# GpSimd multiplies x by 1/rms and ScalarE makes h twice in the first stage; six more filling products at the beginning

## The chip, the cores and the metric

The kernel runs on one core of a Trainium2 chip. The metric is the device time of one execution in microseconds. Before the change three runs gave a median of 972.54 us (971.67 to 973.52). One further execution was profiled; its instructions can be read one by one.

The engines of a core work side by side, each through its own list of instructions in order: TensorE (PE, matrix products; PEld is its weight load), VectorE (DVE), ScalarE (ACT), GpSimd (POOL), and SyncE (SP), which here only issues DMAs. An instruction waits until the semaphores that it names are reached, and everything behind it on its engine waits with it.

## The reference, cut to what matters

A decoder trunk of two layers. Each layer has a feed-forward network (FFN), a token mixer (attention) and a second FFN. Before each of them x is normalised and modulated with a scale and a shift that come from the vector c:

```
def rms_norm(x, g):
    xf = x.astype(jnp.float32)
    y = xf * lax.rsqrt(jnp.mean(xf * xf, axis=-1, keepdims=True) + EPS)
    return (y * g.astype(jnp.float32)).astype(x.dtype)

def modulate(h, shift, scale):
    return h * (1 + scale[:, None, :]) + shift[:, None, :]

def swiglu(h, w_in, w_out):
    g, u = jnp.split(h @ w_in, 2, axis=-1)
    return (jax.nn.silu(g) * u) @ w_out

        mod = c_act @ ada_w[layer] + ada_b[layer]
        sh1, sc1, g1, sh2, sc2, g2, sh3, sc3, g3 = jnp.split(mod, N_MOD, axis=-1)
        h = modulate(rms_norm(x, norm_g[layer, 0]), sh1, sc1)
        x = x + 0.5 * g1[:, None, :] * swiglu(h, ffn_w_in[layer, 0], ffn_w_out[layer, 0])
```

x has 256 positions and 1024 features, the hidden width of the FFN is 2816, and everything is float32. The change concerns the first of these stages alone: h of layer 0's first FFN, with A = g x (1 + scale) and the shift sh, h = x x (1/rms) x A + sh.

## The kernel before

x lies in SBUF with features on the 128 partitions: eight blocks k = 0 to 7 of 128 features by 256 positions. A float32 product is made of three products of reduced precision: each operand is split into a high half and the rest. Of h these are the tiles `HH` and `HL`, of the weights `wh` and `wl`, and `mm3` (line 410) issues wh·HH, wl·HH and wh·HL, in this order, so the third product of each group needs `HL`.

Weights come from HBM through SP's queue in pieces of 128 by 1024 into `raw` (six buffers). ScalarE casts a piece to its high half `wh` (`cp_part`, line 298, six buffers), and VectorE subtracts to get `wl` (`sub_part`, line 310, five buffers); the subtraction frees the `raw` buffer, and SP issues the next load. The modulation is computed on VectorE: `ada_block` (line 196) multiplies a loaded tile `ada` of 128 by 1024 with `cact` and sums over the free axis into one column of `modall`. The block of a scale is followed by a tiny operation that makes the column of A; the block of a shift gives its column directly.

The beginning (lines 900 to 926) loads x, squares it on ScalarE, sums over the features with products against a tile of ones (`psn`), and `rstd_of` (line 452) makes r = 1/rms of it with one ScalarE operation and three on VectorE. `warm(n)` (line 893) issues n products of the ones with themselves; their results are used by nobody. Then the first stage of the FFN begins (line 573). For every block k of x it does, in the order of the code:

- for k > 0: `ada_block` (scale column k), `cp_part`, `ada_block` (shift column k);
- `make_h` (line 467): VectorE makes `ht` = x·A·r in one operation, ScalarE makes `HH` = ht + sh in its high half;
- `sub_part` and `cp_part`: `wl` of the step's first weight piece, `wh` of its second;
- the function that `make_h` returned: VectorE makes `HL` = ht + sh - HH;
- `sub_part`: `wl` of the second piece;
- 16 blocks of weight columns through `mm3`: 48 products of 128x256 into the eight PSUM banks `pf0` to `pf7`.

One such pass is called a step here; the eight steps make the stage. The order on each engine is the order of this code; TensorE goes from step to step as the tiles become ready. Behind the stage the banks are emptied (`evac`: ScalarE's `sg`, VectorE's `hf` and `hidl`, ScalarE's `hidh`), and the next groups of hidden columns go to the banks `pg` and `pu`. For the rest of the kernel a small planner (class `InOrder`, line 54, and `bg`, `fill_act`, `fill_dve`) decides, from estimated costs, between which products a cast, a subtraction or an `ada_block` is placed.

Of the kernel before, what the change touches and what calls it, by code (L numbers as in the profile page):

```python
# [10 lines left out]
F32 = mybir.dt.float32  # L11
F32R = mybir.dt.float32r
BF16 = mybir.dt.bfloat16
AF = mybir.ActivationFunctionType
ALU = mybir.AluOpType
PSUM = bass.MemoryType.PSUM

P = 128
D = 1024
S = 256  # L20
NC = D // P
# [82 lines left out]
def trunk(ctx, tc, a, out):  # L104
    nc = tc.nc
    InOrder.ready = {}
    pe = InOrder(tc, nc.tensor, 0.0, 1 / 2350)
    act = InOrder(tc, nc.scalar, 0.13, 1 / 1200)
    dve = InOrder(tc, nc.vector, 0.08, 1 / 960)
    sp = InOrder(tc, nc.sync, 0.0, 1 / 704)  # L110
    cp_ = ctx.enter_context(tc.tile_pool(name="cp", bufs=1))
# [3 lines left out]
    kp = ctx.enter_context(tc.tile_pool(name="kp", bufs=2))  # L115
    pp = ctx.enter_context(tc.tile_pool(name="pp", bufs=1, space=PSUM))

    def mmbank(name):
        return pp.tile([P, 512], F32, tag="mm", name=name, bufs=4)

    def sbank(name):
        return pp.tile([P, 512], F32, tag="s", name=name, bufs=2)

    def abank(name):
        return pp.tile([P, 512], F32, tag="ta", name=name)

    def bbank(name):
        return pp.tile([P, 512], F32, tag="tb", name=name)
# [17 lines left out]
    x = [xx[:, k] for k in range(NC)]  # L146
# [17 lines left out]
    def table(func):  # L164
        act.preload_act_table(func)


    mods = {}
# [27 lines left out]
    def ada_block():  # L196

        u, i = divmod(ada_done[0], 2)
        if u >= len(ada_list):
            return  # L200
        ada_done[0] += 1
        t = ada_tiles[u]
        m, j = ada_list[u][i]
        if m not in mods:
            mods[m] = [mod_col(), None]
        mt = mods[m][0]
        col = V_ADAB + 2 * u + i
        dve.tensor_tensor_reduce(
            t[:, i], t[:, i], cact, 1.0, vecs[:, col:col + 1], ALU.mult, ALU.add,
            accum_out=mt[:, j:j + 1])  # L210
        kind = m[1] % 3 if m[0] != "kv" else m[1]
        if kind != 0 and m[1] != 5:
            if mods[m][1] is None:
                mods[m][1] = mod_col()
            mx = mods[m][1]
            js = (j, j + 1) if m == (0, 1) else ((j - 3, j + 1) if j % 4 == 3 else None)
            if js is not None:
                js = slice(*js)
                if kind == 1:
                    gc = V_KVN if m[0] == "kv" else V_NORM + (m[0] * 3 + m[1] // 3) * NC  # L220
                    dve.scalar_tensor_tensor(
                        mx[:, js], mt[:, js], 1.0, vecs[:, gc + js.start:gc + js.stop],
                        op0=ALU.add, op1=ALU.mult)
                else:
                    dve.tensor_scalar_mul(mx[:, js], mt[:, js], 0.5)
        if i == 1:
            ada_dma()
# [70 lines left out]
    def cp_part():  # L298

        u = len(his)  # L300
        n = pieces[u][2]
        act.t = max(act.t, used[u - NHI] if u >= NHI else 0.0)
        raw = raws[u]
        if u >= len(pieces) - 6:
            gated[0](raw[:, :n])
        wh = wp.tile([P, WB], F32R, tag="wh", name="wh")[:, shift.get(u, 0):]
        act.plainly(lambda: act.copy(wh[:, :n], raw[:, :n]))
        his.append(wh)

    def sub_part():  # L310

        u = len(los)
        if u == len(his):
            return
        n = pieces[u][2]
        dve.t = max(dve.t, used[u - NLO] if u >= NLO else 0.0)
        wl = wp.tile([P, WB], F32R, tag="wl", name="wl", bufs=NLO)[:, shift.get(u, 0):]
        dve.plainly(lambda: dve.tensor_tensor(wl[:, :n], raws[u][:, :n], his[u][:, :n].bitcast(F32),
                                              op=ALU.subtract))
        los.append(wl)  # L320
        w_dma()
# [80 lines left out]
    def later(n, f):  # L402
        laters.append([n, f])
# [6 lines left out]
    def mm3(ps, w, xx, first, last):  # L410
        (wh, wl), (xh, xl) = w, xx
        mm(ps, wh, xh, start=first, stop=False, skip_group_check=True)
        mm(ps, wl, xh, start=False, stop=False, skip_group_check=True)
        mm(ps, wh, xl, start=False, stop=last, skip_group_check=True)
        work(P)
# [5 lines left out]
    hn = [(HH[:, k, :S], HL[:, k, :S]) for k in range(NC)]  # L421
# [45 lines left out]
    def make_h(k, r, m):  # L467

        A, sh = mods[m[0]][1], mods[m[1]][0]
        t = kp.tile([P, S], F32, tag="ht", name=f"ht{k}")  # L470
        dve.scalar_tensor_tensor(t, x[k], A[:, k:k + 1], r, op0=ALU.mult, op1=ALU.mult)
        hh, hl = hn[k]
        act.activation(hh, t, AF.Identity, bias=sh[:, k:k + 1])
        return lambda: dve.scalar_tensor_tensor(hl, t, sh[:, k:k + 1], hh.bitcast(F32),
                                                op0=ALU.add, op1=ALU.subtract)

    class MakeH:


# [68 lines left out]
    def ffn(l, i, kind, m, nxt, at=2):  # L548
# [24 lines left out]
        if (l, i) == (0, 0):  # L573
            banks = ([mmbank(f"pf{b}") for b in range(4)] + [sbank(f"pf{b}") for b in range(4, 6)]
                     + [abank("pf6"), bbank("pf7")])
            for k in range(NC):
                if k:
                    ada_block()
                    cp_part()
                    ada_block()  # L580
                f = make_h(k, kind, m)
                sub_part()
                cp_part()
                f()
                sub_part()
                blk = take("win0")
                for b in range(4 * K0):
                    mm3(banks[b // 2][:, (b % 2) * 256:(b % 2) * 256 + 256], blk(b * P), hn[k],
                        k == 0 and b % 2 == 0, k == NC - 1)
            table(AF.Silu)  # L590
            cp_part()
            sub_part()
            cp_part()
            sub_part()
            mode[0] = "run"
            for j in range(K0):
                if j < 2:
                    evac(banks[2 * j], banks[2 * j + 1])
                    if j == 0:
                        flush()  # L600
                        flush()
                else:
                    later(2 * j - 2, lambda j=j: evac(banks[2 * j], banks[2 * j + 1]))
            j0 = K0
        elif kind == "late":
            banks = [mmbank("lg0"), mmbank("lg1"), sbank("lu0"), sbank("lu1")]
            r = None
            for kh in range(2):
                blk = take("win")
                for kk in range(4):  # L610
                    k = kh * 4 + kk
                    for b in range(4):
                        mm3(banks[b][:, :SX], blk(kk * 512 + b * P), hx[k], k == 0, k == NC - 1)
                    if k == 2:
                        r = rstd_of(AF.Silu)
                        mh = MakeH(r, m)
                    elif 2 < k < 7:
                        mh.go(2 if k < 6 else 1)
            mh.go(2)
            mode[0] = "run"  # L620
            sg = kp.tile([P, 512], F32, tag="w512a", name="sg")
            hf = kp.tile([P, 512], F32, tag="w512b", name="hf")
            cols = []

            def late_block(b):
                if b == 0:
                    cols.append(late_cols(banks))
                c = cols[0]
                t = kp.tile([P, S], F32, tag="sq", name=f"lt{b}")
                dve.tensor_tensor(t, banks[b][:, :S], r, op=ALU.mult)  # L630
                cs = slice((b % 2) * S, (b % 2) * S + S)
                if b < 2:
                    act.activation(sg[:, cs], t, AF.Silu, bias=c[:, b:b + 1])
                else:
                    dve.scalar_tensor_tensor(hf[:, cs], t, c[:, b:b + 1], sg[:, cs],
                                             op0=ALU.add, op1=ALU.mult)
                if b == 3:
                    hid_out(hf)
            for b in range(4):
                later(2 + b, lambda b=b: late_block(b))  # L640
            j0 = 1
        for j in range(j0, NG):
            pg, pu = mmbank(f"pg{j}"), mmbank(f"pu{j}")
            for kh in range(2):
                blk = take("win")
                for kk in range(4):
                    k = kh * 4 + kk
# [14 lines left out]
        for n in range(NC):  # L662
# [3 lines left out]
            for hf in range(2):  # L666
                blk = take("wout")
                for kk in range(11):
                    k = hf * 11 + kk
# [3 lines left out]
                    hh, hl = hid[k // 2]  # L673
# [219 lines left out]
    def warm(n):  # L893

        pw = bbank("warm")
        for _ in range(n):
            mm(pw[:, :P], ones, ones, start=True, stop=True)
# [24 lines left out]
    ada_block()  # L922
    ada_block()
    rstd = rstd_of(None, [sq4[i][:, h * S:(h + 1) * S] for i in (0, 2) for h in range(2)])
    warm(6)
    cp_part()


# [226 lines left out]
    op, rest = attention_a()  # L1155
# [212 lines left out]
    op, rest = attention_b()  # L1368
# [132 lines left out]
```

## Time and profile before

| | |
|---|---|
| median of three runs | 972.54 us |
| lowest and highest | 971.67 and 973.52 us |
| the profiled execution | 974.37 us, of which 972.5 us are its span (first to last instruction) |
| mean granted clock of TensorE in it | 0.996 |
| PE busy over the span | 960.3 us, 99% |
| DVE busy | 821.7 us, 84% |
| ACT busy | 552.1 us, 57% |
| POOL busy | 68.7 us, 7% |

A row of a timeline gives the start and the duration in microseconds, the engine, the line (99 for all instructions that go through the recording class `InOrder`), the operation, what it writes and reads, how many instructions are merged in it, and in brackets the idle time before it with what ended it. Matmuls are pipelined: their starts are the measure of their pace, and their recorded durations overlap. The rows of busy time by stretch give, after the stretch, the busy time of PE, PEld, DVE, ACT and POOL with the number of instructions, the granted TensorE clock, the busy share of the DMA engines and GB/s. `CUSTOM_DVE_ANT_0` is VectorE's product with a sum behind it, and `DVE_READ_ACCUMULATOR2_ANT` writes that sum out.

### The profile page before, as it was taken

The page shows a single profiled execution, that of the slowest core. Times are in us where ns is not written, and L with a number is a line of the kernel's source. Part 1 is how long each engine was busy: PE and PEld are TensorE (multiplying, and loading weights), DVE is VectorE, ACT ScalarE, POOL GpSimd, SP SyncE. Part 2 cuts the span into 40 slices and gives each one's busy share as a digit, 9 for nine tenths or more (in the row PEclk, how much of TensorE's full clock was granted, in tenths as well). Part 3 has the DMA queues.
Part 4 walks back from the last instruction along what each step waited for, and adds up shares of the span by engine and source line. Part 5 has one row for each costly group of instructions (what it writes and reads, how often), then busy time and mean ns, then how long its engine had stood idle before and what let it go on. Part 6 is the DMA issues. An engine that isn't in the chain of part 4 may idle for free.

```text
span 972.5 us, 20416 instructions
## 1 busy us (share of the span) xinstructions
PE 960.3 (99%) x8076; PEld 933.7 (96%) x8076; DVE 821.7 (84%) x1372; ACT 552.1 (57%) x894; POOL 68.7 (7%) x110
## 2 busy tenths in 40 slices
PE   8999999999999999999999999999999999999997
PEld 6999999998999999999998999999998899999997
DVE  6988979889999999888889988988988799555575
ACT  5366645566787654545577555445567676455432
POOL 0000200000112000000000000000044014300000
PEclk9999999999999999999999999999999999999999
DMA  9997899968856699878959799988895337978651
GB/s 357 415 356 248 333 371 350 332 234 257 333 182 258 190 374 382 334 253 315 326 190 380 280 348 329 371 290 318 321 313 171 109 110 223 273 151 275 186 152 44
DMA packets 69473, 268.22 MB, mean 276 GB/s; under 512 B 9417, under 2 KB 10225, under 8 KB 59266
## 3 DMA queue, kind: packets, MB, share of 16 engines
q1 hardware_dynamic: 66016, 259.69, 75.9%
q0 software_dynamic: 3072, 6.92, 2.4%
q8 instruction: 63, 1.03, 0.4%
q10 hardware_dynamic: 290, 0.32, 0.1%
q14 instruction: 32, 0.26, 0.1%
HBM read 264.75 MB, written 2.66 MB: 275 GB/s over the span
## 4 chain that ended last, share of the span: by engine, by line
PE 96%; DVE 2%; DMA 1%; ACT 0%; issue 0%; SPq 0%; ACTq 0%
PE po L99 25%; PE pg L99 21%; PE pu L99 21%; PE pf L99 5%; PE pv L99 5%; PE pw L99 4%; PE lp L99 4%; PE pqk L99 3%; PE lg L99 1%; PE lq L99 1%; PE lu L99 1%; PE pk L99 1%; PE wb L99 1%; DVE ada L99 1%; DMA x<-in_x 1%; PE sb L99 1%
## 5 line engine op out<-in xcount | busy, mean ns | idle before, releaser
L99 ACT CAST wh<-raw 128x1024 fp32r<-128x1024 f32 (+1 forms) x360 | 347.1, 975 | 211.1 <-PE pu L99 76.8
L99 DVE TENSOR_TENSOR wl<-raw,wh 128x1024 fp32r<-128x1024 f32 (+1 forms) x360 | 399.6, 1128 | 68.9 <-ACT sg L99 19.0
L99 DVE CUSTOM_DVE_ANT_0 ada<-ada,cact,vecs 128x1024 f32<-128x1024 f32 x160 | 203.3, 1277 | 0.0
L99 PE MATMUL pg<-HH,wl 128*128 128x256 f32 x608 | 168.1, 277 | 0.4 <-DVE wl L99 0.4
L99 PE MATMUL pg<-HH,wh 128*128 128x256 f32 x608 | 168.0, 276 | 0.0
L99 PE MATMUL pg<-HL,wh 128*128 128x256 f32 x608 | 167.9, 276 | 0.0
L99 PE MATMUL pu<-HH,wh 128*128 128x256 f32 x608 | 167.9, 276 | 0.0
L99 PE MATMUL pu<-HL,wh 128*128 128x256 f32 x608 | 167.9, 276 | 0.0
L99 PE MATMUL pu<-HH,wl 128*128 128x256 f32 x608 | 167.9, 276 | 0.0
L99 PE MATMUL po<-hidh,wh 128*128 128x256 f32 x528 | 145.7, 276 | 0.0
L99 PE MATMUL po<-hidh,wl 128*128 128x256 f32 x528 | 145.7, 276 | 0.0
L99 PE MATMUL po<-hidl,wh 128*128 128x256 f32 x528 | 145.7, 276 | 0.0
L99 PEld LDWEIGHTS pg<-HH,wl 128*128 128x128 f32 x608 | 114.1, 188 | 0.9 <-DVE wl L99 0.8
L99 PEld LDWEIGHTS pg<-HH,wh 128*128 128x128 f32 x608 | 114.1, 188 | 0.7 <-issue 0.6
L99 PEld LDWEIGHTS pu<-HH,wl 128*128 128x128 f32 x608 | 114.1, 188 | 0.0
L99 PEld LDWEIGHTS pg<-HL,wh 128*128 128x128 f32 x608 | 114.1, 188 | 0.0
L99 PEld LDWEIGHTS pu<-HH,wh 128*128 128x128 f32 x608 | 114.1, 188 | 0.0
L99 PEld LDWEIGHTS pu<-HL,wh 128*128 128x128 f32 x608 | 114.1, 188 | 0.0
L99 PEld LDWEIGHTS po<-hidl,wh 128*128 128x128 f32 x528 | 99.1, 188 | 0.0
L99 PEld LDWEIGHTS po<-hidh,wh 128*128 128x128 f32 x528 | 99.1, 188 | 0.0
L99 PEld LDWEIGHTS po<-hidh,wl 128*128 128x128 f32 x528 | 99.1, 188 | 0.0
L99 ACT CAST hidh<-hf 128x512 fp32r<-128x512 f32 x44 | 27.3, 621 | 41.7 <-DVE hf L99 41.7
(224 smaller groups left out, 1855.0 us busy)
## 6 DMA issues: line engine op xcount, KB each, us to landing
raw<-in_win SPq DMA_DIRECT2D x176, 512.0 KB, 6.8
ada<-in_ada SPq DMA_DIRECT2D x79, 1024.0 KB, 7.2
raw<-in_wout SPq DMA_DIRECT2D x48, 384.0 KB, 5.5
raw<-in_wout SPq DMA_DIRECT2D x48, 320.0 KB, 5.3
raw<-in_wqk SPq DMA_DIRECT2D x16, 512.0 KB, 5.6
raw<-in_wo SPq DMA_DIRECT2D x16, 512.0 KB, 5.2
raw<-in_wlast SPq DMA_DIRECT2D x16, 512.0 KB, 4.2
raw<-in_wv SPq DMA_DIRECT2D x8, 512.0 KB, 6.2
```

Of the source, the lines that this page charges most:

```text
L99: return self.tc.keep_in_program_order(f(*args, **kw))
```

## The change

In the first stage, for the blocks k = 1 to 7, the product x·r is taken from VectorE and made by GpSimd, all seven right behind one another as soon as r exists, into seven tiles `xr` that borrow the memory of the later `hidh1` to `hidh7`. ScalarE then computes A·xr + sh twice: once into `HH` (high half), once into `ht` in float32. VectorE's operation for `HL` becomes a plain subtraction, ht - HH. Block 0 is made as before. The filling products before the stage become twelve instead of six.

```
+    def spread_r(k, r):
+
+        xr = cp_.tile([P, 512], F32, tag=f"hidh{k}", name=f"xr{k}")[:, :S]
+        nc.gpsimd.tensor_tensor(xr, x[k], r, op=ALU.mult)
+        return xr
+
+    def make_h_from(k, xr, m):
+
+        A, sh = mods[m[0]][1], mods[m[1]][0]
+        hh, hl = hn[k]
+        act.activation(hh, xr, AF.Identity, bias=sh[:, k:k + 1], scale=A[:, k:k + 1])
+        t = kp.tile([P, S], F32, tag="ht", name=f"ht{k}")
+        act.activation(t, xr, AF.Identity, bias=sh[:, k:k + 1], scale=A[:, k:k + 1])
+        return lambda: dve.tensor_tensor(hl, t, hh.bitcast(F32), op=ALU.subtract)
+
...
-                f = make_h(k, kind, m)
+                if k == 0:
+                    f = make_h(k, kind, m)
+                    xrs = [None] + [spread_r(j, kind) for j in range(1, NC)]
+                else:
+                    f = make_h_from(k, xrs[k], m)
                 sub_part()
                 cp_part()
                 f()
...
-    warm(6)
+    warm(12)
```

The first place is VectorE's list from `ht` of step 0 to the end of step 1, before the change (`ISA ada` is the product with a sum of an `ada_block`, `ISA modall` the row that writes the sum out):

```order
L99 SCALAR_TENSOR_TENSOR ht_171<-x,modall,r_148 128x256
L99 TENSOR_TENSOR wl<-raw,wh 128x1024
L99 SCALAR_TENSOR_TENSOR HL<-ht_171,modall,HH 128x256
L99 TENSOR_TENSOR wl<-raw,wh 128x1024
L99 ISA ada,modall<-ada,cact,vecs 128x1024
L99 ISA modall 128x1
L99 SCALAR_TENSOR_TENSOR modall<-modall,vecs 128x1
L99 ISA ada,modall<-ada,cact,vecs 128x1024
L99 ISA modall 128x1
L99 SCALAR_TENSOR_TENSOR ht_240<-x,modall,r_148 128x256
L99 TENSOR_TENSOR wl<-raw,wh 128x1024
L99 SCALAR_TENSOR_TENSOR HL<-ht_240,modall,HH 128x256
```

and the same stretch after it, from the first `ada` sum of step 1 on:

```order
L99 ISA ada,modall<-ada,cact,vecs 128x1024
L99 ISA modall 128x1
L99 SCALAR_TENSOR_TENSOR modall<-modall,vecs 128x1
L99 ISA ada,modall<-ada,cact,vecs 128x1024
L99 ISA modall 128x1
L99 TENSOR_TENSOR wl<-raw,wh 128x1024
L99 TENSOR_TENSOR HL<-ht_261,HH 128x256
L99 TENSOR_TENSOR wl<-raw,wh 128x1024
```

`ht` of step 1 has left VectorE's list, and `HL` reads two tiles and no column; so in each of the steps 1 to 7, and nothing else has moved on this engine.

The second place is ScalarE's list from `HH` of step 0 to that of step 2, before the change (a row with x2 is the second piece of one step and the first of the next):

```order
L99 ACTIVATE HH<-ht_171,modall 128x256
L99 CAST wh<-raw 128x1024 x2
L99 ACTIVATE HH<-ht_240,modall 128x256
L99 CAST wh<-raw 128x1024 x2
L99 ACTIVATE HH<-ht_309,modall 128x256
```

and after it (the numbered `xr` are GpSimd's products):

```order
L99 ACTIVATE HH<-ht_177,modall 128x256
L99 CAST wh<-raw 128x1024 x2
L99 ACTIVATE HH<-xr_180,modall 128x256
L99 ACTIVATE ht_261<-xr_180,modall 128x256
L99 CAST wh<-raw 128x1024 x2
L99 ACTIVATE HH<-xr_182,modall 128x256
L99 ACTIVATE ht_330<-xr_182,modall 128x256
```

`ht` now stands between `HH` and the cast of the step's second weight piece.

The third place is GpSimd's list behind the program's start, where there was nothing ahead of `udram` before; after the change:

```order
L480 ISA
L480 TENSOR_TENSOR xr_180<-x,r_148 128x256
L480 TENSOR_TENSOR xr_182<-x,r_148 128x256
L480 TENSOR_TENSOR xr_184<-x,r_148 128x256
L480 TENSOR_TENSOR xr_186<-x,r_148 128x256
L480 TENSOR_TENSOR xr_188<-x,r_148 128x256
L480 TENSOR_TENSOR xr_190<-x,r_148 128x256
L480 TENSOR_TENSOR xr_192<-x,r_148 128x256
L970 DMA udram<-ut 8x383
```

The seven products stand one behind the other. On TensorE only the number of filling products differs, and SP's list is the same as before.

## The prediction

> **What bounds the kernel now.** I read the page's chain of work first, then the PE's own timeline at the beginning, then the stages' busy time with the granted clock, and last VectorE's and ScalarE's timelines in the first stage.
>
> ```profile
> PE 96%; DVE 2%; DMA 1%; ACT 0%; issue 0%; SPq 0%; ACTq 0%
> ```
>
> The time is TensorE's time: 96% of the chain that ended last. An edit in the first stage counts only by what it does to the moment at which TensorE leaves that stage. So the PE timeline there, from the filling products to the first product of the next stage:
>
> ```profile
> 11.18 1.50 PE L99 MATMUL warm<-ones 128*128 128x128 f32 x12
> 15.19 0.38 PE L99 MATMUL pf<-HH,wh 128*128 128x256 f32 x1 [2.51 <-ACT HH L99]
> 15.79 0.38 PE L99 MATMUL pf<-HH,wl 128*128 128x256 f32 x1 [0.21 <-DVE wl L99]
> 16.18 0.55 PE L99 MATMUL pf<-HL,wh 128*128 128x256 f32 x1
> ...
> 62.70 0.28 PE L99 MATMUL pf<-HL,wh 128*128 128x256 f32 x1
> 62.82 0.27 PE L99 MATMUL pg<-HH,wh 128*128 128x256 f32 x1
> ```
>
> TensorE stands still for 2.5 us, starts at 15.19, is held once for the first `wl` and once for the first `HL`, and runs without a break from 16.18 to 62.82. Its pace in that run, by busy time in stretches (the second of these rows counts the products of the stage alone; the column behind the counts is the granted clock):
>
> ```profile
> 16.25:19.66 3.41, 3.41 (x16) 3.41 (x17) 3.38 (x5) 1.04 (x1) 0.00 (x0) 0.50 1.00 414
> 25.00:60.00 35.00, 35.00 (x300) 1.00 1.02 413
> ```
>
> In the second row 300 products touch 35.0 us, the two at the edges only in part: one per 0.1175 us, so a step of 48 takes 5.64 us. In the first row the clock is half: 3.41 us give the work of 1.7 us. The half clock follows the pause at 12.7 to 16.2, and it costs 1.7 us. Check: 16.18 + 46 x 0.1175 + 1.7 + 7 x 5.64 = 62.8, as seen.
>
> VectorE runs beside it. One step, then the last `HL` of the stage:
>
> ```profile
> 13.65 0.42 DVE L99 SCALAR_TENSOR_TENSOR r<-ra,r 128x256 f32<-128x256 f32 x1
> 14.11 0.48 DVE L99 SCALAR_TENSOR_TENSOR ht<-x,modall,r 128x256 f32<-128x256 f32 x1
> 14.51 1.22 DVE L99 TENSOR_TENSOR wl<-raw,wh 128x1024 fp32r<-128x1024 f32 x1
> 15.65 0.48 DVE L99 SCALAR_TENSOR_TENSOR HL<-ht,modall,HH 128x256 fp32r<-128x256 f32 x1
> 16.11 1.23 DVE L99 TENSOR_TENSOR wl<-raw,wh 128x1024 fp32r<-128x1024 f32 x1
> 17.25 1.28 DVE L99 CUSTOM_DVE_ANT_0 ada<-ada,cact,vecs 128x1024 f32<-128x1024 f32 x1
> ...
> 19.86 0.08 DVE L99 DVE_READ_ACCUMULATOR2_ANT modall<- 128x1 f32 x1
> 19.86 0.48 DVE L99 SCALAR_TENSOR_TENSOR ht<-x,modall,r 128x256 f32<-128x256 f32 x1
> 20.25 1.22 DVE L99 TENSOR_TENSOR wl<-raw,wh 128x1024 fp32r<-128x1024 f32 x1
> 21.39 0.48 DVE L99 SCALAR_TENSOR_TENSOR HL<-ht,modall,HH 128x256 fp32r<-128x256 f32 x1
> 21.85 1.23 DVE L99 TENSOR_TENSOR wl<-raw,wh 128x1024 fp32r<-128x1024 f32 x1
> ...
> 55.83 0.48 DVE L99 SCALAR_TENSOR_TENSOR HL<-ht,modall,HH 128x256 fp32r<-128x256 f32 x1
> ```
>
> VectorE has no idle time here, and its step is (55.83 - 21.39) / 6 = 5.74 us, longer than TensorE's 5.64. It does not hold TensorE, because TensorE lost 1.7 us to the clock: the last step starts at 62.82 - 5.64 = 57.18, wants `HL` with its third product at 57.4, and `HL` is there at 56.31. The margin is 1.1 us, less than the 1.7 us of the clock. So neither edit alone could bring all of it.
>
> **The change part by part.**
>
> *The six fillers.* Twelve records took 1.50 us, so twelve more run from 12.68 to about 14.1, before `HH` lets the first product go at 15.19. They delay nothing. If they keep the clock, step 0 ends at 16.18 + 46 x 0.1175 = 21.6 instead of 23.3. No row shows how much work keeps it, so the value lies between 0 and -1.7 us.
>
> *VectorE's part.* Seven `ht` go, 0.40 us each by the starts 19.86 and 20.25. Seven `HL` become plain subtractions, for which the nearest row is this one:
>
> ```profile
> 967.16 0.41 DVE L99 TENSOR_TENSOR x<-x,rows 128x256 f32<-128x256 f32 x1
> ```
>
> That is 0.07 us less than 0.48. Counted from the end of the second `ada` sum, `HL` comes 0.47 us earlier, and VectorE's own work per step falls to some 5.2 us. That gain meets a new wait.
>
> *ScalarE's part.* The same `ht` now stands on ScalarE, between `HH` and the cast of the step's second weight piece:
>
> ```profile
> 20.37 0.51 ACT L99 ACTIVATE HH<-ht,modall 128x256 fp32r<-128x256 f32 x1 [1.86 <-DVE ht L99]
> 20.79 1.03 ACT L99 CAST wh<-raw 128x1024 fp32r<-128x1024 f32 x1
> ```
>
> `HH` needs the shift column, so it can start when the accumulator is read, 19.94 + 0.04. Then `HH` 0.42 (start to start), `ht` the same, the cast 1.03 and 0.04 for the signal: the second `wl` can start at 21.89. Before it starts at 21.85. VectorE's step therefore stays at 5.78 us: it now ends with a wait on ScalarE's cast, and queued behind that waiting `wl` are both `ada` sums on which the next `HH` depends. It is a ring through both engines; the removed 0.5 us turn into idle time. What is left of the gain is `HL` 0.47 us earlier within the step.
>
> *GpSimd's part.* Seven multiplies are queued without a wait between them, and they ask from about 14.15, when r is there (13.65 + 0.42). No row shows them in this stage. Elsewhere GpSimd multiplies or adds tiles of the same size, beside VectorE:
>
> ```profile
> 58.66 2.36 DVE L99 TENSOR_TENSOR wl<-raw,wh 128x1024 fp32r<-128x1024 f32 x2 [1.14 <-ACT wh L99]
> 723.34 2.89 DVE L99 TENSOR_TENSOR wl<-raw,wh 128x1024 fp32r<-128x1024 f32 x2
> 724.28 0.87 POOL L1253 TENSOR_TENSOR d<-d,tri 128x256 f32<-128x256 f32 x1 [1.65 <-DMA d<-fdram]
> 779.95 0.73 POOL L448 TENSOR_TENSOR acc<-sq,sq 128x256 f32<-128x256 f32 x1 [24.45 <-ACT sq L99]
> 780.00 0.97 DVE L99 SCALAR_TENSOR_TENSOR HL<-x,modall,HH 128x256 fp32r<-128x256 f32 x1
> 741.29 1.42 POOL L1253 TENSOR_TENSOR d<-d,tri 128x256 f32<-128x256 f32 x2 [2.79 <-DMA d<-fdram]
> 741.30 0.42 DVE L99 CUSTOM_DVE_ANT_0 d<-sb,d 128x256 f32<-128x256 f32 x1
> ```
>
> Two `wl` with a GpSimd operation between them take 2.89 us instead of 2.36, and that operation 0.87 instead of 0.73: it waited for the first `wl` to finish, then the second `wl`, already queued, waited for it. An `HL` begun 0.05 us behind a GpSimd operation takes 0.97 instead of 0.48. So the two take turns, and one GpSimd operation costs a busy VectorE about 0.53 us. In the last two rows nothing is lost: that VectorE operation reads `sb` from PSUM, and `d` alone from SBUF. In the first stage VectorE's operations read two tiles from SBUF and stand back to back, so a GpSimd operation slips in at nearly each change. For the `ada` sum (`ada` and `cact`, both in SBUF) no row has it beside such a multiply: between 0, as for `d<-sb,d`, and 0.53, as for `wl`, I take 0.53, since its operands lie as those of `wl`.
>
> The Trainium skill, "SBUF — State Buffer", section "Who interferes with whom", says that a VectorE instruction with two SBUF inputs contends with a GpSimd instruction that reads SBUF, and that the lock holds for the whole instruction. The rows above agree (0.53 and 0.49 us); by that rule the `ada` sum is held too, and the sum stays as it follows here.
>
> Up to `HL` of step 1 there are the changes ht/wl, wl/HL, HL/wl, wl/ada, ada/modall, modall/ada and wl/HL: seven for seven multiplies. The tiny `modall` operation and the sum behind it lie closer together than GpSimd's cadence of about 0.7 us, so one may be saved; I take six and a half, 3.45 us, between 0 (all hidden) and 3.7.
>
> *The sum at TensorE.* The first `HL` comes two holds later, so the unbroken run starts at 16.18 + 1.06 = 17.24, and step 0 ends at 22.65 with the full clock, at 24.35 with the half. `HL` of step 1 is ready at 21.87 - 0.47 + 3.45 = 24.85; a step's first two products (0.235 us) do not need it, so step 1 starts at 24.85 + 0.05 - 0.235 = 24.67 either way. That is the point: TensorE waits there for VectorE, and what the fillers save is waited away. In step 1 the holds hide the cast, so `HL` of step 2 follows after 5.26, then five times 5.78: 59.0 for the last one. Step 7 starts at 58.8 (TensorE alone would be at 24.67 + 6 x 5.64 = 58.5) and ends at 64.45, against 62.82: **+1.6 us**.
>
> Behind the stage the shift has to pass one narrow place:
>
> ```profile
> 57.58 2.00 ACT L99 CAST wh<-raw 128x1024 fp32r<-128x1024 f32 x2
> 60.94 0.68 DVE L99 TENSOR_TENSOR hf<-sg,pf 128x512 f32<-128x512 f32 x1
> ```
>
> `hf` empties the second bank at 61.6, and TensorE wants it six products after 62.82, at 63.5. That margin of 1.9 us shrinks to a few tenths, since ScalarE's line there moves by some 3.2 us and TensorE's by 1.6; I cost it at nothing, and up to 0.5 if it is gone. After that TensorE is the chain again and carries 1.6 us to the end. The profiled execution took 974.37 us (span 972.5 and 1.9 around it) and would become 976.0. It lies 1.8 us above the median of the runs, 972.54, a difference that I carry over: 972.54 + 1.6 = **974.2 us**.
>
> **The rivals.**
>
> *A: as summed.* 974.2 us, with six or seven holds and the narrow place 973.8 to 975.0. For it: the turns at 723 and 780.
>
> *B: the `ada` sum is not held.* Only three holds lie on the path, 1.6 us: `HL` of step 1 at 23.0, the last at 57.7. TensorE ends at 63.1 with the full clock, or at 24.35 + 7 x 5.64 = 63.8 with the half: +0.3 to +1.0, some 973.2. For it: the 0.42 us at 741.30; against it: that one reads PSUM.
>
> *C, the slower side: the clock falls once more.* If the fillers keep the clock at first, TensorE stands from 22.65 to 24.67. The clock fell after a pause of 2.5 us with two short ones behind it; a pause of 2.0 us may do it too. Then another 1.7 us go, with no margin to absorb them: 975.9. It decides if a pause of 2.0 us is enough. The Trainium skill, "TensorE: Matmul & The Clock Gate", section "Why this matters for your kernels", warns of pauses over about 3 us; by that rule C does not occur, but the trace disagrees, with half clock after 2.5 us.
>
> *D: GpSimd costs nothing.* The last `HL` comes at 21.40 + 6 x 5.78 = 56.1, TensorE ends at 61.55 with the full clock: -1.3, 971.3. Against it: the pairs of rows above.
>
> *E: the change does what it says.* No holds and no ring: VectorE's step falls to 5.2, TensorE alone decides, 21.6 + 7 x 5.64 = 61.1: -1.7, 970.8. Against it: the holds and the cast behind `ht`. That VectorE is relieved in fact is the claim that I doubt.
>
> **How the numbers follow.** A 0.48, B 0.13, C 0.17, D 0.12, E 0.10. About 0.2%, 1.95 us, is what a measurement of this kernel tells from no change. Slower by more: C, and about four tenths of A, whose upper part lies over 974.5 and more so where the runs before had kept their clock: 0.36. Faster by more: only E with a lucky start, 0.06. Within: 0.58. The range goes from D, 971.3, to C, 975.9; E's end and the worst of C are left out.
>
> **What would show it.** GpSimd's multiplies from 14.15 to about 24, several of them well over 0.73 us; the first `wl` at about 1.75 us; TensorE's run from 17.2; a wait of TensorE on `HL` before 24.9; VectorE idle for ScalarE's cast in each later step, with 5.78 us from `HL` to `HL`; the first product of `pg` at 64.4. It is wrong if the `ada` sums keep 1.28 us beside GpSimd (B), if a second stretch of half clock shows after 23 (C), or if `pg` starts before 62.8 (D, E).

## The result and the profile after

| | before | after |
|---|---|---|
| median of six runs | 972.24 us | 976.80 us |
| lowest and highest | 971.67 and 973.52 us | 976.53 and 980.92 us |
| the profiled execution | 974.37 us, span 972.5 | 980.92 us, span 979.1 |

The kernel became slower: the ratio of after to before is 1.0052, with a 95% interval from 1.0035 to 1.0069, that is by 3.4 to 6.7 us. The forecast was 974.2 us, at most 975.9. Ratios here and below are estimated from all the runs and differ a little from the quotient of the medians. One run of the kernel before, among the 35 beside e1 to e4, took 1775.31 us at a granted clock of 0.80; it counts neither in the ratios nor in the spread given below.

The page's chain of the changed kernel, by engine:

```profile
PE 88%; DVE 7%; ACT 2%; DMA 2%; issue 1%; SPq 0%; ACTq 0%; DVEq 0%
```

TensorE had 96% of the chain and VectorE 2%; now VectorE has 7%. The chain goes through VectorE in the first stage, with ScalarE's cast once in each later step, to 59.6 us, and through TensorE from there on. The PE timeline of the changed kernel (start, duration, what; in brackets the idle time before and what ended it) begins and leaves the stage like this:

```profile
14.35 0.39 PE L99 MATMUL pf<-HH,wh 128*128 128x256 f32 x1 [1.39 <-ACT HH L99]
15.47 0.38 PE L99 MATMUL pf<-HH,wl 128*128 128x256 f32 x1 [0.74 <-DVE wl L99]
16.34 0.58 PE L99 MATMUL pf<-HL,wh 128*128 128x256 f32 x1 [0.49 <-DVE HL L99]
...
65.17 0.27 PE L99 MATMUL pg<-HH,wh 128*128 128x256 f32 x1
```

Starts of two executions can't be compared as they stand, since r is ready at another moment in each (loads at the beginning): 14.07 us in the profile of before, 12.25 + 0.42 = 12.67 here. So the measure used from here on is the **stretch**, from the end of r to the first product of `pg`: 62.82 - 14.07 = 48.75 us before, 65.17 - 12.67 = 52.50 us after. VectorE's timeline of the changed kernel shows where it went:

```profile
12.25 0.42 DVE L99 SCALAR_TENSOR_TENSOR r<-ra,r 128x256 f32<-128x256 f32 x1
12.71 1.05 DVE L99 SCALAR_TENSOR_TENSOR ht<-x,modall,r 128x256 f32<-128x256 f32 x1
13.68 1.74 DVE L99 TENSOR_TENSOR wl<-raw,wh 128x1024 fp32r<-128x1024 f32 x1
15.34 0.94 DVE L99 SCALAR_TENSOR_TENSOR HL<-ht,modall,HH 128x256 fp32r<-128x256 f32 x1
16.21 1.75 DVE L99 TENSOR_TENSOR wl<-raw,wh 128x1024 fp32r<-128x1024 f32 x1
17.88 1.75 DVE L99 CUSTOM_DVE_ANT_0 ada<-ada,cact,vecs 128x1024 f32<-128x1024 f32 x1
19.56 0.07 DVE L99 DVE_READ_ACCUMULATOR2_ANT modall<- 128x1 f32 x1
19.67 0.57 DVE L99 SCALAR_TENSOR_TENSOR modall<-modall,vecs 128x1 f32<-128x1 f32 x1
20.17 1.84 DVE L99 CUSTOM_DVE_ANT_0 ada<-ada,cact,vecs 128x1024 f32<-128x1024 f32 x1
21.94 0.08 DVE L99 DVE_READ_ACCUMULATOR2_ANT modall<- 128x1 f32 x1
21.94 1.22 DVE L99 TENSOR_TENSOR wl<-raw,wh 128x1024 fp32r<-128x1024 f32 x1
23.24 0.42 DVE L99 TENSOR_TENSOR HL<-ht,HH 128x256 fp32r<-128x256 f32 x1
24.17 1.23 DVE L99 TENSOR_TENSOR wl<-raw,wh 128x1024 fp32r<-128x1024 f32 x1 [0.51 <-ACT wh L99]
25.32 1.28 DVE L99 CUSTOM_DVE_ANT_0 ada<-ada,cact,vecs 128x1024 f32<-128x1024 f32 x1
...
29.23 0.43 DVE L99 TENSOR_TENSOR HL<-ht,HH 128x256 fp32r<-128x256 f32 x1
...
59.15 0.42 DVE L99 TENSOR_TENSOR HL<-ht,HH 128x256 fp32r<-128x256 f32 x1
```

Two things are to be seen. From 12.71 to 22 seven operations of VectorE each take some half a microsecond more than their like at other times, `ada` too (1.75 and 1.84, against 1.28 at 25.32): the holds. Only the reading of the accumulator is not longer (0.07). From `HL` of step 2 at 29.23 to that of step 7 at 59.15 there are five steps of 5.98 us; before, a step took 5.74. GpSimd's timeline and the waits of VectorE between 20 and 62 us (total, times, longest) give the two causes:

```profile
12.75 8.18 POOL L480 TENSOR_TENSOR xr<-x,r 128x256 f32<-128x256 f32 x7 [12.30 <-DVE r L99]
```

```profile
DVE wl L99 <- ACT wh L99: 3.6, 7, 0.5
```

The multiplies run from the end of r for 8.18 us, 1.17 each on the mean, and the holds fall in the same time. Behind that, VectorE waits 0.51 us for ScalarE's cast in each of the seven steps. ScalarE's timeline shows the cause of this second wait:

```profile
22.11 0.60 ACT L99 ACTIVATE HH<-xr,modall 128x256 fp32r<-128x256 f32 x1 [4.97 <-DVE modall L99]
22.62 0.59 ACT L99 ACTIVATE ht<-xr,modall 128x256 f32<-128x256 f32 x1
23.11 1.99 ACT L99 CAST wh<-raw 128x1024 fp32r<-128x1024 f32 x2
```

`HH` and `ht` with a column as scale and another as bias last 0.60 and 0.59 us and follow each other after 0.51 and 0.49; `HH` of before, with the bias column alone, lasted 0.51 and was followed after 0.42.

### The profile page after: what moved, and what is told of

It is laid out like the page before. It is cut to its first block, busy times and chain, and to the rows that moved or that the text cites. A ratio compares the mean times of both kernels' runs of the same rounds, so it can differ in the third digit from the quotient of the medians.

```text
span 979.1 us, 20460 instructions
## 1 busy us (share of the span) xinstructions
PE 966.8 (99%) x8088; PEld 939.1 (96%) x8088; DVE 824.0 (84%) x1365; ACT 556.2 (57%) x901; POOL 77.6 (8%) x117
## 4 chain that ended last, share of the span: by engine, by line
PE 88%; DVE 7%; ACT 2%; DMA 2%; issue 1%; SPq 0%; ACTq 0%; DVEq 0%
PE po L99 24%; PE pg L99 21%; PE pu L99 21%; PE pv L99 5%; PE pw L99 4%; PE lp L99 4%; PE pqk L99 3%; DVE ada L99 3%; DVE wl L99 2%; PE lq L99 1%; PE pk L99 1%; DVE HL L99 1%; DMA raw<-in_wkk 1%; PE wb L99 1%; PE sb L99 1%
```

## The experiments

Three theories stood against each other at first: the multiplies hold VectorE (**holds**), the second `ht` on ScalarE makes VectorE wait for the cast (**ring**), and the clock or the fillers decide (**clock**). Profiles are compared by the stretch. Times are compared by the lowest of the runs where there are some: executions of one and the same kernel spread by up to 12 us on some chips, and in the profiles most of that arises behind this stage: from `pg` to the end the twelve take 909.5 to 920.4 us (last section). This blurs the medians more than the lowest.

### e1: the fillers alone

On the kernel before:

```
-    warm(6)
+    warm(12)
```

> The kernel before with twelve filling products instead of six, nothing else. In the profiles so far TensorE's first stage took, from the end of the operation that makes r to the first product of pg, 48.75 us before and 52.50 us after the change; this stretch is the measure, since it leaves out the luck of the first loads. Theory F (the fillers keep the clock): no half clock at 16 to 20 us, the stretch 47.6 us (VectorE then decides), total 1.1 us below before. Theory N (they buy nothing, because the pause behind them stays too long, as the profile after the change shows half clock again): 48.75 us and the same total within 0.5 us. I hold N for likelier.

Median 972.91 us beside 972.50 of the kernel before, ratio 0.9996 (0.9965 to 1.0026); lowest 971.82 beside 971.75. No half clock occurs in its profile before the end of the kernel, and the stretch is 47.65 us.

### e2: all but the fillers

On the changed kernel:

```
-    warm(12)
+    warm(6)
```

> The changed kernel with six filling products again: GpSimd's multiplies and ScalarE's second operation alone. Theory HR (GpSimd's turns plus the ring through ScalarE make the loss, the fillers nothing): the stretch from r to pg is 52.5 us as after the whole change, total 4 to 4.6 us above before. If the twelve fillers made part of the loss, or saved part of it, the stretch is apart from 52.5 by that part (1.7 us, if they had saved the clock).

Median 977.32 us, ratio 1.0046 (1.0016 to 1.0076), lowest 976.48. The half clock lasts from 14.53 to 21.36 (the row is by stretch: PE, PEld, DVE, ACT, POOL busy, granted clock, DMA, GB/s), twice as long as in the first profiles of before and after, and the stretch is 52.31 us, 0.2 less than with the twelve fillers. So these runs show no worth of the fillers with the change or without it, and the loss lies in the other part.

```profile
14.53:21.36 6.83, 5.80 (x23) 5.21 (x24) 6.79 (x7) 2.13 (x3) 6.77 (x6) 0.50 1.03 419
```

### e3: no multiplies

On the changed kernel; the factor 1/rms is left out of h in blocks 1 to 7:

```
     def spread_r(k, r):
-        xr = cp_.tile([P, 512], F32, tag=f"hidh{k}", name=f"xr{k}")[:, :S]
-        nc.gpsimd.tensor_tensor(xr, x[k], r, op=ALU.mult)
-        return xr
+        return x[k]
```

> The changed kernel without GpSimd's multiplies: ScalarE reads x itself for the blocks 1 to 7, so that h of these blocks lacks the factor 1/rms. All else stays, the ring through ScalarE too. Theory HR: the holds are gone, HL of step 1 is ready 7.5 us after r (11.0 after the change, 7.8 before); the step from HL to HL stays 5.99 us; the stretch from r to pg is 49.0 us, 3.5 less than after the change, total about 1 us above before. Rival R (the ring alone made the loss): the stretch stays near 52.5 us. Rival H (the holds alone): 48.7 us or less and the step back at 5.7 us or less.

Median 972.81 us, ratio 1.0002 (0.9975 to 1.0029), lowest 972.35. The stretch is 48.44 us. The first steps on VectorE are back to their old durations, but the wait remains, as two neighbouring steps of its VectorE timeline show:

```profile
20.58 1.22 DVE L99 TENSOR_TENSOR wl<-raw,wh 128x1024 fp32r<-128x1024 f32 x1 [0.52 <-ACT wh L99]
...
26.51 1.23 DVE L99 TENSOR_TENSOR wl<-raw,wh 128x1024 fp32r<-128x1024 f32 x1 [0.51 <-ACT wh L99]
```

5.93 us lie between them. So even with GpSimd's work gone, giving `ht` to ScalarE in this order of the code makes VectorE's step longer (5.93 against 5.74), not shorter. `HL` of step 1 ends 7.45 us after r, 0.34 earlier than before; `HL` of step 7 at 43.04, 0.8 later.

### e4: no second activation

On the changed kernel; the shift is left out of `HL` in blocks 1 to 7, which VectorE makes from `xr` in one operation:

```
-        t = kp.tile([P, S], F32, tag="ht", name=f"ht{k}")
-        act.activation(t, xr, AF.Identity, bias=sh[:, k:k + 1], scale=A[:, k:k + 1])
-        return lambda: dve.tensor_tensor(hl, t, hh.bitcast(F32), op=ALU.subtract)
+        return lambda: dve.scalar_tensor_tensor(hl, xr, A[:, k:k + 1], hh.bitcast(F32),
+                                                op0=ALU.mult, op1=ALU.subtract)
```

> The changed kernel without ScalarE's second operation: VectorE makes HL of the blocks 1 to 7 from GpSimd's xr, as xr times A minus HH, which leaves the shift out of HL. GpSimd's seven multiplies stay. Theory HR: the ring is gone and the holds stay: HL of step 1 about 10.9 us after r, then 5.2 to 5.4 us from HL to HL for VectorE, so that TensorE's own 5.64 decide from step 1 on; the stretch from r to pg is 50.2 us, 2.3 less than after the change, total about 2 us above before. Rival R (the ring alone): 48.7 us or less. Rival H (the holds alone): 52.5 us as after the change.

Lowest 973.54 us, median 976.40, ratio 1.0028 (1.0001 to 1.0055). `HL` of step 1 ends 10.91 us after r, so the holds are all there; then the step is 5.50 us and the waits for the cast shrink to 1.1 us in all. Without the second activation on ScalarE most of the ring is gone (six steps of 5.50 instead of 5.99), and by the lowest times 1.8 of the 4.9 us remain, since the holds are still paid.

### e5: the cast moved ahead

On the changed kernel, whole computation. ScalarE's cast of the step's second weight piece is put in front of `HH`:

```
                 if k:
                     ada_block()
                     cp_part()
+                    cp_part()
                     ada_block()
...
                 sub_part()
-                cp_part()
+                if k == 0:
+                    cp_part()
                 f()
```

> The changed kernel, complete, with both casts of a step ahead of the second ada block, so that ScalarE has HH and ht alone to make once the shift column is there. GpSimd's multiplies stay. Theory HR: the ring opens, VectorE no longer waits 0.51 us per step for the cast, its step falls from 5.99 to about 5.5 us; HL of step 1 stays near 10.9 us after r; TensorE's own pace decides from step 1 on: from r to pg 49.2 to 50.3 us, 2.2 to 3.2 less than after the change, and total 2 to 3 us above before. If the longer step came from slower VectorE work instead of the wait for the cast, the step stays at 5.99 and the stretch at 52.5.

The wait is gone; VectorE's timeline between two `HL`:

```profile
23.65 0.43 DVE L99 TENSOR_TENSOR HL<-ht,HH 128x256 fp32r<-128x256 f32 x1
23.99 1.22 DVE L99 TENSOR_TENSOR wl<-raw,wh 128x1024 fp32r<-128x1024 f32 x1
25.13 1.28 DVE L99 CUSTOM_DVE_ANT_0 ada<-ada,cact,vecs 128x1024 f32<-128x1024 f32 x1
...
29.04 0.42 DVE L99 TENSOR_TENSOR HL<-ht,HH 128x256 fp32r<-128x256 f32 x1
```

The step is 5.39 us, and the stretch falls from 52.50 to 49.05. Lowest time 973.30 us beside 971.72 of the kernel before on this chip: of the loss of 4.9 us (lowest times of the first table) 1.6 remain. By medians it is 977.16 beside 976.12, ratio 1.0002 (0.9975 to 1.0029), too blurred to say more. So 3.3 us can be had back by the order of the code. The holds stay: `HL` of step 1 still ends 11.02 us after r.

### e6: three multiplies

On the changed kernel, whole computation; blocks 4 to 7 are made as before:

```
-                if k == 0:
+                if k == 0 or k > 3:
                     f = make_h(k, kind, m)
-                    xrs = [None] + [spread_r(j, kind) for j in range(1, NC)]
+                    if k == 0:
+                        xrs = [None] + [spread_r(j, kind) for j in range(1, 4)]
```

> The changed kernel with GpSimd's multiply and ScalarE's second operation for the blocks 1 to 3 alone; the blocks 4 to 7 as before the change. Theory HR, priced per multiply: three holds of 0.53 us lie ahead of HL of step 1, so it is ready 7.8 - 0.4 + 1.6 = 9.0 us after r (11.0 with seven); two ring steps of 5.99, the others 5.75; the stretch from r to pg is 49.7 us, total about 2 us above before. If the loss ahead of step 1 came all at once (GpSimd's first use, say) and not by the multiply, HL of step 1 stays near 11 us.

`HL` of step 1 ends 9.00 us after r, between 7.45 with no multiply (e3) and 10.99 with seven: 1.55 for three and 3.54 for seven, 0.52 and 0.51 each. The price goes with the number. Of the six steps behind it two take 5.99 us and three 5.74, as expected; the one from block 3 to block 4, where the old form begins again, takes 6.22 and was not expected. Stretch 50.14 us, lowest time 974.30, median 978.25, ratio 1.0009 (0.9979 to 1.0039).

### e7 and e8: both kernels once more

No edit; one execution of each, to see whether the profile of before that the prediction started from was a usual one.

> The kernel before, unchanged, for a second profile. The question is whether the half clock at 16 to 20 us in its first profile is what its runs usually have. If it is: half clock again and 48.75 us from r to pg. If that profile was an unlucky one: no half clock, and 47.6 us, as with twelve fillers.

> The changed kernel, unchanged, for a second profile. Theory HR: HL of step 1 at 11.0 us after r, 5.99 us from HL to HL, 52.3 to 52.5 us from r to pg, with or without half clock, since TensorE waits for VectorE. The stretch of slower products at 805 to 916 us in the first profile (117.8 ns each instead of 113.3) is not expected again.

e7 took 972.14 us, e8 977.52. The kernel before, by stretch (PE, PEld, DVE, ACT, POOL busy, granted clock, DMA, GB/s), and where its stage ends:

```profile
14.82:18.23 3.41, 3.41 (x15) 3.29 (x16) 3.38 (x6) 1.28 (x2) 0.00 (x0) 0.50 1.05 428
25.00:44.00 19.00, 19.00 (x170) 18.98 (x168) 18.89 (x31) 9.07 (x12) 0.00 (x0) 1.00 1.02 415
```

```profile
60.72 0.28 PE L99 MATMUL pg<-HH,wh 128*128 128x256 f32 x1
```

It has the half clock, as in the first profile, and yet its stretch is 60.72 - 13.06 (the end of its r) = 47.66 us: the same as that of e1, which kept its clock (47.65), and 1.1 less than the 48.75 of the first profile. The second row tells why: 168 whole products in 19.0 us, 0.113 us each, where the first profile had 0.1175. At 0.113 a step of TensorE is 5.44 us, TensorE catches up what the clock cost, and VectorE's 5.74 sets the end. In the first profile the half clock and the slower pace came together, and only so was TensorE 1.1 us later than VectorE would have let it be. e8 has no half clock at all and still a stretch of 52.51 us, as the first profile of the changed kernel with half clock (52.50). In neither kernel does the half clock by itself decide.

### e9 and e10: the price alone, and the change without it

e9 is the kernel before with seven multiplies whose results nobody reads:

```
                 f = make_h(k, kind, m)
+                if k == 0:
+                    for j in range(1, NC):
+                        xr = cp_.tile([P, 512], F32, tag=f"hidh{j}", name=f"xr{j}")[:, :S]
+                        nc.gpsimd.tensor_tensor(xr, x[j], kind, op=ALU.mult)
```

> The kernel before, complete and unchanged on every other engine, with GpSimd's seven multiplies added and their results unused. Nothing waits for GpSimd by a semaphore. Theory HR (turns at SBUF): each multiply still holds VectorE 0.53 us; HL of step 1 is ready 7.8 + 3.7 = 11.5 us after r instead of 7.8; the step stays 5.74; from r to pg 47.65 + 3.7 = 51.4 us, and the undisturbed runs 3.7 us above those of before. Rival: if VectorE or ScalarE lost the time by waiting for xr, this kernel takes what before takes, 47.65 us.

Lowest 975.45 us beside 972.05, median 980.04 beside 976.17, ratio 1.0043 (1.0009 to 1.0078). Four rows of its VectorE timeline, with r at the same moment as in e7:

```profile
12.63 0.42 DVE L99 SCALAR_TENSOR_TENSOR r<-ra,r 128x256 f32<-128x256 f32 x1
...
14.06 1.74 DVE L99 TENSOR_TENSOR wl<-raw,wh 128x1024 fp32r<-128x1024 f32 x1
...
18.26 1.75 DVE L99 CUSTOM_DVE_ANT_0 ada<-ada,cact,vecs 128x1024 f32<-128x1024 f32 x1
...
23.84 0.47 DVE L99 SCALAR_TENSOR_TENSOR HL<-ht,modall,HH 128x256 fp32r<-128x256 f32 x1
```

The same `HL` in e7:

```profile
20.38 0.48 DVE L99 SCALAR_TENSOR_TENSOR HL<-ht,modall,HH 128x256 fp32r<-128x256 f32 x1
```

23.84 against 20.38: seven multiplies that nobody waits for cost VectorE 3.46 us, 0.49 each, and the steps behind them are unchanged (5.74). The stretch is 51.12 us, 3.46 more, and the lowest time is 3.4 more: the hold goes through to the end in full.

e10 is e5 with `spread_r` returning `x[k]` as in e3; it leaves the factor 1/rms out of h in blocks 1 to 7.

> The changed kernel with both casts ahead of the second ada block and without GpSimd's multiplies (ScalarE reads x itself, so h of the blocks 1 to 7 lacks 1/rms): VectorE's relief with neither holds nor ring, which no complete kernel here has. Theory HR: HL of step 1 about 7.4 us after r, VectorE's step 5.4, which is about TensorE's fast pace (48 products of 0.1133 us, 5.44 us): from r to pg 45.4 us at that pace and with the full clock, up to 47.2 with half clock or slow pace; undisturbed runs 1 to 2 us below before. If it stays at 47.6, VectorE was not what bounds the stage.

The stretch is 45.88 us, 1.8 less than before. Lowest time 971.17 us beside 972.05; median 975.80 beside 976.17, ratio 0.9988 (0.9946 to 1.0030), no difference that these runs can tell. That is the most these edits could bring: x·r made by nobody and the cast moved out of the way. ScalarE's casts then begin to wait for the loads of the weight pieces: 12 times between 20 and 62 us, 10.5 us in all, against once and 0.7 us in the first profile of before. A hold costs 0.5 us, and a step with the cast ahead saves 5.74 - 5.39 = 0.35, so a block whose product goes to GpSimd loses more on VectorE than it gains. No version with the whole computation beat the kernel before.

| kernel | stretch | `HL` of step 1 ends after r | step | `HL` of step 7 |
|---|---|---|---|---|
| before (first profile) | 48.75 | 7.79 | 5.74 | 42.24 |
| e7 before | 47.66 | 7.79 | 5.75 | 42.28 |
| e1 before, twelve fillers | 47.65 | 7.79 | 5.74 | 42.25 |
| after | 52.50 | 10.99 | 5.99 | 46.91 |
| e8 after | 52.51 | 11.01 | 5.99 | 46.93 |
| e2 after, six fillers | 52.31 | 10.98 | 5.99 | 46.92 |
| e3 no multiplies | 48.44 | 7.45 | 5.93 | 43.04 |
| e4 no second activation | 50.26 | 10.91 | 5.50 | 43.91 |
| e5 cast ahead | 49.05 | 11.02 | 5.39 | 43.34 |
| e6 three multiplies | 50.14 | 9.00 | 5.91 | 44.47 |
| e9 unused multiplies | 51.12 | 11.26 | 5.74 | 45.72 |
| e10 cast ahead, no multiplies | 45.88 | 7.45 | 5.42 | 39.94 |

(The step is the mean of the six from `HL` of step 1 to that of step 7.)

## Why the prediction was wrong, point by point

The likeliest case, A, named the right mechanisms, and the time came out beyond the range because two sizes were off, one in the sum and one in what it was added to.

**The fillers** were given 0 to -1.7 us and said to be waited away in step 1. So it was: the changed kernel has the same stretch with six fillers (e2, 52.31) and with twelve, with half clock (52.50) and without (e8, 52.51).

**The holds** were the doubtful term, and it stood. `HL` of step 1 was forecast at 24.85, 10.78 us after r; it ended at 10.99. The `ada` sum is held (1.75 and 1.84 instead of 1.28), which refutes rival B; the multiplies were held too, by more than the rows at 723 and 780 had shown: 1.17 us each on the mean. The 0.53 per hold taken from the pairs of `wl` and `HL` came out as 0.49 (e9) to 0.52 (e6). The rule of the Trainium skill, "SBUF — State Buffer", section "Who interferes with whom", agrees here also for the product with a sum, and the 0.42 us of `d<-sb,d` was no guide to it. The text let the holds begin behind the first `ht`; that `ht` was held as well (1.05 us), so the first `HL` met three holds instead of two, and the seventh multiply ended at 20.93, beside the second `ada` sum.

**The ring is the step that failed, by its size.** The text has "VectorE's step therefore stays at 5.78 us" and "In step 1 the holds hide the cast, so `HL` of step 2 follows after 5.26". The first used the 0.42 us that followed a `HH` with one column; the new `HH` and `ht` use two columns and cost 0.51 and 0.49, and `HH` started 0.17 behind the start of the accumulator's reading instead of 0.12. 0.09 + 0.07 + 0.05 = 0.21, and 5.78 became 5.99. The second failed because all seven holds lay before `wl` of step 1 at 21.94, which took its usual 1.22; so this step waited 0.51 us like all others, and `HL` of step 2 followed after 29.23 - 23.24 = 5.99, not 5.26. Together 0.73 + 5 x 0.21 = 1.8 us at the last `HL`, and with the 0.2 of the holds and 0.1 in the last step it makes the 2.1 by which the stretch exceeded the forecast (52.50 against 64.45 - 14.07 = 50.38). e4 and e5 take the ring away in two ways, and the step falls to 5.50 and 5.39; e3 keeps it without the holds, and it is 5.93.

**The base is the other step that failed.** The +1.6 us was counted from the profiled execution and carried to the median. That assumed that the profiled stage was a usual one and that the 1.8 us by which that execution lay above the median had nothing to do with it. e7 shows that 1.1 us of it lay in this very stage: TensorE's pace there was 0.1175 us on top of the half clock, and the end was TensorE's. "So neither edit alone could bring all of it" rested on that end, too; in e1 and e7 VectorE sets it, with no margin, so that a delay on VectorE goes through in full (3.46 us at `HL` and in the stretch of e9), and e1, fillers alone, brings nothing. From a stretch of 47.66 the forecast one, 50.38, would have been +2.7.

The sum of it: 1.6 + 2.1 + 1.1 = 4.8 us, measured 4.6 by the medians and 4.9 by the lowest times. **The narrow place** behind the stage (`hf`) was given nothing, up to 0.5 us, and it cost nothing: counted from the first product of `pg`, the first 200 products start at the same moments within 0.02 us in after, e2, e8, e1 and e7. From `pg` to the end the profiles e2 and e8 take 910.1 to 910.3 us where e1 and e7 take 909.5 to 909.7. That 0.5 us arises far behind this place: where a single wait of TensorE is longer than in e1, the largest is 492 us behind `pg` in e2 (0.7 us) and 740 us behind it in e8 (0.2 us). Why it is longer there stays open.

**The rivals.** C did not occur: no second stretch of half clock in after or e8. D and E, GpSimd free or everything as said, are e10's world: it ends 1.8 us earlier, but only with no multiplies and with the cast moved. That this is close to the -1.7 of E is luck: E had the stage end at 61.1 - 14.07 = 47.0 us after r, counted down from 48.75; e10 ends at 45.88, counted down from 47.66. The chance of slower, 0.36, was too small for a kernel in which VectorE sets the end of the stage.

## What to carry to other kernels

Work handed from a saturated VectorE to GpSimd is paid by VectorE once per instruction, here 0.5 us for a tile of 128x256, whichever of VectorE's operations with two operands in SBUF it met, from the product with a sum down to the 128x1 operation on `modall` (0.57 instead of 0.16). It must save VectorE more than that, and a 0.4 us `ht` does not. When an operation moves to another engine, write out the loop of waits through both engines with the durations of the very forms that will run there, and for every step of the loop, the first one too. Before a difference is added to a median, look whether the profiled execution is like the median one in the stage that the change touches: a second profile of the unchanged kernel would have shown it.

## What the runs showed of the hardware that I had not expected

TensorE runs the same stream of products at one of two paces at the full clock. The busy time by stretch in the last FFN of the first profile of each kernel, TensorE alone (busy, products, granted clock, DMA, GB/s), first before, then after:

```profile
810.00:895.00 85.00, 85.00 (x752) 1.00 0.87 235
```

```profile
814.00:900.00 86.00, 86.00 (x733) 1.00 0.85 227
```

85.0 us for 750 whole products are 0.113 us each, 86.0 for 731 are 0.118, with no idle time and the clock at 1.00 in both. Over those 750 products that makes 3.2 us. It is the greater part of why the profiled execution of after took 980.92 us: from `pg` to the end it needed 913.9 us, 4.3 more than e7.

It also explains the spread of the profiles. Counted in their traces, of the 7656 products behind the first of `pg`, those that start 0.1155 to 0.121 us behind the one before are 762 in e7, 1633 in after, 2117 in e9 and 3173 in e6, and `pg` to the end takes 909.6, 913.9, 916.0 and 920.4 us. From e7 to e6 that is 2411 products at 4.4 ns more, 10.6 us, and the time is 10.8 us longer. The runs of the kernel before that lie near 972, 976 and 982 us on some chips are likely spread by the same thing, but those executions left no trace.

The pace mostly stays the same through a stage (0.1175 all through the first stage of before). In the first stage of after, where TensorE waits once in each step, it is another behind five of the seven waits: 0.113 in the steps 0, 2, 4 and 5, 0.118 in the steps 1, 3, 6 and 7. What sets it stays open; nothing in the granted clock or the DMA share of the two rows above tells them apart.

The half clock, too, came and went with the same program: 3.4 us of it in the first profile of after and none in e8 up to the end of the kernel, both with twelve fillers and with the waits of TensorE 1.39, 0.74 and 0.49 us there, 0.73, 0.74 and 0.48 here. The fillers do bear on it: all four profiles with six of them (before, e2, e7, e9) have 3.4 or 6.8 us of half clock at the beginning of the stage, of the eight with twelve only after and e6 have it, 3.4 us each. The Trainium skill, "TensorE: Matmul & The Clock Gate", section "Why this matters for your kernels", warns of pauses over about 3 us; the profile of after shows the half clock behind none longer than 1.4 us between products.
